# Layer 1's modulation of the context stream only where it is used, and output projections in blocks of 512 columns by 512 rows

## The chip, the cores and the metric

The kernel runs on one core of a Trainium2 chip. The metric is the device time of one execution in microseconds (us). TensorE (PE) multiplies matrices from SBUF into the eight banks of PSUM; VectorE (DVE), ScalarE (ACT) and GpSimd (POOL) work on elements; SyncE (SP) issues the transfers from and to HBM. The order of the instructions on each engine is fixed when the program is built.

## The reference

Two layers of a diffusion backbone work on 256 context tokens and 256 latent tokens of 1024 channels. Of the context, layer 1 uses only what its token mixer reads; the output is the latent stream.

```python
for l in range(DEPTH):                       # DEPTH = 2
    need_ctx = l < DEPTH - 1
    m_l = split(silu(c)     @ w_ada[l] + b_ada[l], 6)    # w_ada[l]: 1024 x 6144
    m_c = split(silu(c_ctx) @ w_ada[l] + b_ada[l], 6)
    h_l = modulate(rms_norm(x,   norm_g[l, 0]), m_l[0], m_l[1])   # h * (1 + scale) + shift
    h_c = modulate(rms_norm(ctx, norm_g[l, 0]), m_c[0], m_c[1])
    y_l, y_c = token_mixer(h_l, h_c, ...)    # ends in merged @ w_out[l], 1024 x 1024
    x = x + m_l[2] * rms_norm(y_l, norm_g[l, 1])
    h_l = modulate(rms_norm(x, norm_g[l, 2]), m_l[3], m_l[4])
    x = x + m_l[5] * rms_norm(relu(h_l @ w_mlp_up[l])**2 @ w_mlp_down[l], norm_g[l, 3])
    if need_ctx:                             # not in layer 1
        ...the same for ctx with m_c[2] to m_c[5]
return x
```

## The kernel before

**Precision.** Each float32 operand of a projection is split in two parts, `hi` (rounded) and `lo` (the rest), and a product takes three matmuls: hi by hi, hi by lo, lo by hi. For weights ACT writes `hi` (line 226) and DVE `lo` (line 227), four pieces of 128x512 for each weight block. A block has 2048 columns in SBUF (1 MB from HBM, two transfers of 512 KB) and there are two block buffers in `whl`; block n+2 is split when block n has been read.

**Two forms of projection.** `mm_cm` (lines 248 to 250) holds weights in the array and moves activations past them: 512 tokens at a time in layer 0, mostly 256 in layer 1. `mm_tm` (lines 260 to 262) holds the activations of one token tile (`tt`, 128 tokens: 0 and 1 are context, 2 and 3 latent) and moves the weights. `tm_out` uses it for `w_out` and for the MLP's second matrix, called the down projection here.

**tm_out.** A block is 1024 rows (8 tiles of `k`) by 256 columns. For each block and each token tile 24 matmuls of 256 columns sum into half a PSUM bank; then DVE adds the result to `y` (line 652), or ACT copies it (655) where it is the first. In a last pass ACT squares it and sums the squares (657) and DVE multiplies by the gate (659). `seqs` lists which token tiles go through which blocks together. When a tile has all its columns, `after` runs: `post` (629 to 633) adds the normalized result to `x`, and, where a next stage follows, `prenorm` (transposes, line 581) and `modulate` (596 to 605) make its input `h`. The MLP goes in four quarters `qd` of 1024 hidden channels: the up projection by `cm_blocks` (its `relu2` at lines 1317 to 1320 ends in a DVE subtraction that writes `lo`), then the down projection, summed over the quarters in `y`.

**Modulation of layer 1.** `w_ada[1]` is worked off during layer 0's MLP: 48 steps (3 groups `g` of 2048 columns, 2 halves, 8 row tiles), two to each weight block. A step loads 512 KB and runs one DVE multiply-add of 128x1024 for each stream (lines 400, 403). After eight steps `ada_sum` sums over the partitions with matmuls against ones (412), transposes (419) and adds the bias. Group 0 holds the first shift and scale, groups 1 and 2 the rest.

**Order.** The program is written in the order of the layers; `high_priority` marks splits and evictions, and a scheduler then sets each engine's order at build time.

## Time and profile before

| | |
|---|---|
| median of 3 runs | 1625.68 us (1623.34 to 1628.14) |
| the profiled execution | 1622.66 us, of which 1620.9 us are its span |
| busy: PE, DVE, ACT, POOL | 1569.2, 1091.5, 782.5, 387.8 us |
| mean TensorE clock granted | 0.986 of full speed |
| transfers | 220.26 MB, mean 136 GB/s |

The span runs from the first to the last instruction. In it, the stages that the change touches are these: `w_out` of layer 0 from 597.5 to 647 us; the four down projections of layer 0 from 697.8, 792.9, 885.9 and 980.5 us on; `w_out` of layer 1 from 1391.8 to 1418.2 us; the four down projections of layer 1 from 1453.0, 1499.0, 1545.1 and 1591.2 us on, the last of which ends the program.

### The profile page before, as it was taken

Reading aid. Unit: us, or ns where it says so; the run is one execution under the profiler, and the core shown is the slowest. Engines: PE = TensorE matmul, PEld = TensorE weight load, DVE = VectorE, ACT = ScalarE, POOL = GpSimd, SP = SyncE. Lnnn points to the kernel's source line nnn. Section 1 sums busy time; section 2 is a strip of 40 time slices with the busy share of each in tenths; the row PEclk is TensorE's granted clock in tenths of the full one; section 3 lists DMA queues with packets and bytes.
Section 4 is the critical chain, followed back from the end, with each engine's and each line's share of the span. In section 5 each row is a group of like instructions: output and inputs, shape, how many; then the busy total and the mean of one; then the engine's idle time right before and its main releaser. Section 6 shows DMA issues by size and latency. Waiting matters only on the chain.

```text
span 1620.9 us, 30093 instructions
## 1 busy us (share of the span) xinstructions
PE 1569.2 (97%) x11806; PEld 1401.7 (86%) x11806; DVE 1091.5 (67%) x1994; ACT 782.5 (48%) x1648; POOL 387.8 (24%) x419
## 2 busy tenths in 40 slices
PE   6999999999999999999999999999998999989998
PEld 4788888887777789888898989999897999989998
DVE  4655544676576578687878756776668788765555
ACT  4443433455444457533323146644455656666554
POOL 1142415050510001310102011364455350211001
PEclk9999999999999999999999999999999999989999
DMA  9723243324332346466556534432434254446662
GB/s 282 230 79 118 80 130 117 92 66 130 129 93 53 117 141 195 147 189 188 173 178 195 156 104 133 129 118 73 124 104 105 66 162 113 156 131 182 183 182 92
DMA packets 234270, 220.26 MB, mean 136 GB/s; under 512 B 24400, under 2 KB 226320, under 8 KB 234128
## 3 DMA queue, kind: packets, MB, share of 16 engines
q1 hardware_dynamic: 234128, 218.34, 45.1%
q8 instruction: 92, 1.51, 0.4%
q14 instruction: 50, 0.41, 0.1%
HBM read 217.26 MB, written 1.05 MB: 135 GB/s over the span
## 4 chain that ended last, share of the span: by engine, by line
PE 84%; DVE 4%; POOL 4%; DMA 2%; ACT 2%; issue 2%; SPq 1%; DVEq 0%; POOLq 0%; ACTq 0%
PE b L248 15%; PE b L249 15%; PE b L250 15%; PE b L260 9%; PE b L261 9%; PE b L262 9%; DMA arf<-in_w_ada_dram 1%; POOL arf L906 1%; PE b L364 1%; POOL arf L796 1%; PE b L1109 1%; PE b L936 1%; PE b L1096 1%; DVE whl L227 1%; PE b L937 1%
## 5 line engine op out<-in xcount | busy, mean ns | idle before, releaser
L227 DVE TENSOR_TENSOR whl<-raw,whl 128x512 fp32r<-128x512 f32 x588 | 431.9, 755 | 213.0 <-ACT whl L226 201.0
L226 ACT CAST whl<-raw 128x512 fp32r<-128x512 f32 x588 | 356.1, 619 | 247.5 <-PE b L262 111.8
L248 PE MATMUL b<-h,whl 128*128 128x512 f32 (+1 forms) x1296 | 448.1, 347 | 1.1 <-ACT arf L951 0.6
L250 PE MATMUL b<-h,whl 128*128 128x512 f32 (+1 forms) x1296 | 445.4, 344 | 0.9 <-DVE whl L227 0.8
L249 PE MATMUL b<-h,whl 128*128 128x512 f32 (+1 forms) x1296 | 444.7, 343 | 0.0
L248 PEld LDWEIGHTS b<-h,whl 128*128 128x128 f32 x1296 | 247.7, 191 | 33.4 <-ACT whl L226 2.1
L250 PEld LDWEIGHTS b<-h,whl 128*128 128x128 f32 x1296 | 246.8, 191 | 29.4 <-issue 1.6
L249 PEld LDWEIGHTS b<-h,whl 128*128 128x128 f32 x1296 | 247.1, 191 | 28.1 <-issue 2.4
L262 PE MATMUL b<-whl,arr 128*128 128x256 f32 x768 | 215.9, 284 | 1.9 <-DVE arr L1320 1.9
L261 PE MATMUL b<-whl,arr 128*128 128x256 f32 x768 | 217.5, 284 | 0.0
L260 PE MATMUL b<-whl,arr 128*128 128x256 f32 x768 | 217.5, 284 | 0.0
L1319 POOL TENSOR_TENSOR arf<-arf 128x256 f32<-128x256 f32 (+1 forms) x68 | 62.3, 916 | 427.7 <-ACT arr L1318 424.1
L260 PEld LDWEIGHTS b<-whl,arr 128*128 128x128 f32 x768 | 147.5, 192 | 1.4 <-DVE arf L652 0.8
L262 PEld LDWEIGHTS b<-whl,arr 128*128 128x128 f32 x768 | 146.8, 192 | 2.1 <-DVE arr L1320 2.1
L261 PEld LDWEIGHTS b<-whl,arr 128*128 128x128 f32 x768 | 147.5, 192 | 0.1
L260 PE MATMUL b<-whl,h 128*128 128x256 f32 x512 | 146.6, 288 | 0.0
L261 PE MATMUL b<-whl,h 128*128 128x256 f32 x512 | 146.0, 286 | 0.0
L262 PE MATMUL b<-whl,h 128*128 128x256 f32 x512 | 144.7, 285 | 0.0
L906 POOL TENSOR_TENSOR arf<-arf,cst 32x256 f32<-32x256 f32 x104 | 94.3, 907 | 192.7 <-ACT arf L951 71.0
L454 POOL TENSOR_TENSOR sm<-sm,nhalf 128x1 f32<-128x1 f32 (+2 forms) x42 | 33.2, 794 | 345.2 <-DVE sm L629 247.2
L403 DVE SCALAR_TENSOR_TENSOR arf<-arf,CA 128x1024 f32<-128x1024 f32 x84 | 109.3, 1345 | 4.8 <-DMA arf<-in_w_ada_dram 4.8
L260 PEld LDWEIGHTS b<-whl,h 128*128 128x128 f32 x512 | 98.6, 193 | 3.2 <-ACT arf L740 0.8
(224 smaller groups left out, 2504.3 us busy)
## 6 DMA issues: line engine op xcount, KB each, us to landing
raw<-in_w_in_dram SPq DMA_DIRECT2D x110, 512.0 KB, 3.9
arf<-in_w_ada_dram SPq DMA_DIRECT2D x80, 512.0 KB, 4.7
raw<-in_w_mlp_down_dram SPq DMA_DIRECT2D x72, 512.0 KB, 3.7
raw<-in_w_mlp_up_dram SPq DMA_DIRECT2D x64, 512.0 KB, 3.9
raw<-in_w_out_dram SPq DMA_DIRECT2D x24, 512.0 KB, 3.6
arf<-in_w_ada_dram SPq DMA_DIRECT2D x32, 256.0 KB, 5.8
raw<-in_w_branch_dram SPq DMA_DIRECT2D x16, 512.0 KB, 4.2
raw<-in_w_in_dram SPq DMA_DIRECT2D x32, 128.0 KB, 3.3
```

Source lines behind the costliest of these rows:

```text
L226: self.behind(ops, lambda: nc.scalar.copy(r32(h), src))
L227: self.split_op = self.behind(ops, lambda: nc.vector.tensor_tensor(out=r32(l), in0=src, in1=h, op=ALU.subtract))
L248: nc.tensor.matmul(ps, wh, xh[:, t0:t0 + n], start=start and k == 0, stop=False)
L249: nc.tensor.matmul(ps, wh, xl[:, t0:t0 + n], start=False, stop=False)
L250: nc.tensor.matmul(ps, wl, xh[:, t0:t0 + n], start=False, stop=stop and k == nk - 1)
L260: nc.tensor.matmul(ps, xh, wh, start=start and k == 0, stop=False)
L261: nc.tensor.matmul(ps, xh, wl, start=False, stop=False)
L262: nc.tensor.matmul(ps, xl, wh, start=False, stop=stop and k == nk - 1)
L403: self.nc.vector.scalar_tensor_tensor(out=a[:, :], in0=raw[:, :], scalar=ca[:, k, s:s + 1], in1=a[:, :], op0=ALU.mult, op1=ALU.add)
L454: self.nc.gpsimd.tensor_tensor(out=r, in0=ms, in1=self.nhalf[:, 0:cols], op=ALU.pow)
L906: nc.gpsimd.tensor_tensor(out=b[o, 0:LAT], in0=x[i], in1=self.cst[i, C_RS:C_RS + LAT], op=ALU.mult)
L1319: nc.gpsimd.tensor_tensor(out=r[:, c], in0=r[:, c], in1=r[:, c], op=ALU.mult)
```

## The change

A block in `tm_out` is now 512 rows (4 tiles of `k`) by 512 columns, again 2048 columns in SBUF. A sum fills a whole PSUM bank and takes two blocks (`kh` 0 and 1): all token tiles of a sequence go through the first block, each in a bank of its own, and then through the second; where `whole` is set (the last columns of layer 1), both blocks are loaded and the tiles go through both in turn. Evictions have 512 columns (`finish`), and the squares of a token are two sums in place of four. For groups 1 and 2 of layer 1's modulation only the latent stream is multiplied, summed and transposed; the loads stay.

```diff
--- before.py
+++ after.py
@@ -135,7 +135,7 @@
         self.oml = const("oml", 8)
         self.nhalf = const("nhalf", 8)
         self.ones = const("ones", 32)
-        self.yss = const("yss", 20)
+        self.yss = const("yss", 12)
         self.sm_t = const("sm", 512)
         self.sm_i = 0
         self.raw = const("raw", RAWS * 1024)
@@ -374,7 +374,7 @@
             while len(raws) < min(n + 1 + ahead, len(todo)):
                 raws.append(self.ada_load(l, *todo[len(raws)]))
             g, half, k = todo[n]
-            self.ada_acc(raws[n], k, acc)
+            self.ada_acc(raws[n], k, acc, 1 if l == DEPTH - 1 and g else 2)
             if k == 7:
                 self.ada_sum(l, g, half, acc)
                 acc.clear()
@@ -389,11 +389,11 @@
             self.nc.sync.dma_start(raw[:, :].rearrange("p (j c) -> p j c", j=4), src)
         return raw
 
-    def ada_acc(self, raw, k, acc):
+    def ada_acc(self, raw, k, acc, streams):
 
         ca = self.CA.rearrange("p (k m) -> p k m", m=32)
         if k == 0:
-            acc += [self.A.get(2) for _ in range(2)]
+            acc += [self.A.get(2) for _ in range(streams)]
         for s, a in enumerate(acc):
             with self.tc.issue_after(self.split_op.ins):
                 if k == 0:
@@ -413,15 +413,16 @@
                                  a[:, j * 256:j * 256 + 256], start=True, stop=True)
             a.free()
         t = self.A.get(1)
-        nc.vector.tensor_copy(t[:, :], ps)
+        n = 2 * len(acc)
+        nc.vector.tensor_copy(t[:, 0:n * 128], ps[:, 0:n * 128])
         p2 = self.mps()
-        for c in range(4):
+        for c in range(n):
             nc.tensor.transpose(p2[:, c * 128:c * 128 + 128], t[:, c * 128:c * 128 + 128], self.ident)
         t.free()
         qs = slice(2 * half, 2 * half + 2)
         out = self.M[l].rearrange("p (s g j q) -> p s g j q", s=2, g=3, j=4)[:, :, g, :, qs]
         bb = self.bT[:, l * 48 + g * 16:l * 48 + g * 16 + 16].rearrange("p (j q) -> p j q", j=4)[:, :, qs]
-        for s in range(2):
+        for s in range(len(acc)):
             nc.vector.tensor_tensor(out=out[:, s], in0=view(p2, s * 256, [(32, 4), (128, 2)]), in1=bb, op=ALU.add)
 
     def ada_done(self, l, g, qs=range(4), p2=None):
@@ -459,7 +460,7 @@
         nc = self.nc
         part = lambda t: t if q is None else t.rearrange("p (a q) -> p a q", a=2)[:, :, q]
         res = []
-        for s in range(2):
+        for s in range(1 if sub and l == DEPTH - 1 else 2):
             S = self.sb[:, ((l * 2 + sub) * 2 + s) * 8:][:, 0:8]
             g = self.prm[:, l * 32 + sub * 16:l * 32 + sub * 16 + 8]
             nc.vector.scalar_tensor_tensor(out=part(S), in0=part(self.mvec(l, s, 3 * sub + 1)), scalar=1.0, in1=part(g),
@@ -638,26 +639,38 @@
 
         nc = self.nc
         junk = self.A.get(1)
-        left = {tt: 4 for tt in y}
-        for tts, blocks in seqs:
-            blks = [(b, self.wblock(w, r0, 8, b * 256, 256)) for b in blocks]
-            for tt in tts:
-                for b, blk in blks:
-                    ps = self.dps()
-                    self.mm_tm(ps[:, 0:256], blk, 8, 0, 256, act, tt)
-                    o = y[tt][:, b * 256:b * 256 + 256]
-                    with self.hp():
-                        src = ps[:, 0:256]
-                        if add:
-                            nc.vector.tensor_tensor(out=o, in0=src, in1=o, op=ALU.add)
-                            src = o
-                        elif not gains:
-                            nc.scalar.copy(o, src)
-                        if gains:
-                            nc.scalar.activation(junk[:, 0:256], src, AF.Square, scale=D ** -0.5,
-                                                 accum_out=yss[tt][:, b:b + 1])
-                            nc.vector.tensor_tensor(out=o, in0=src, in1=gains(tt)[:, b * 256:b * 256 + 256], op=ALU.mult)
-                left[tt] -= len(blks)
+        left = {tt: 2 for tt in y}
+
+        def finish(tt, b, ps):
+            o = y[tt][:, b * 512:b * 512 + 512]
+            with self.hp():
+                src = ps
+                if add:
+                    nc.vector.tensor_tensor(out=o, in0=src, in1=o, op=ALU.add)
+                    src = o
+                elif not gains:
+                    nc.scalar.copy(o, src)
+                if gains:
+                    nc.scalar.activation(junk[:, :], src, AF.Square, scale=D ** -0.5, accum_out=yss[tt][:, b:b + 1])
+                    nc.vector.tensor_tensor(out=o, in0=src, in1=gains(tt)[:, b * 512:b * 512 + 512], op=ALU.mult)
+            left[tt] -= 1
+
+        for tts, halves, whole in seqs:
+            for b in halves:
+                ps = {}
+                order = [(kh, tt) for kh in range(2) for tt in tts]
+                blks = {}
+                if whole:
+                    order = [(kh, tt) for tt in tts for kh in range(2)]
+                    blks = {kh: self.wblock(w, r0 + kh * 512, 4, b * 512, 512) for kh in range(2)}
+                for kh, tt in order:
+                    if kh not in blks:
+                        blks[kh] = self.wblock(w, r0 + kh * 512, 4, b * 512, 512)
+                    if not kh:
+                        ps[tt] = self.dps()
+                    self.mm_tm(ps[tt], blks[kh], 4, 0, 512, act, tt, kt0=kh * 4, start=not kh, stop=kh == 1)
+                    if kh:
+                        finish(tt, b, ps[tt])
             for tt in tts:
                 if gains and left[tt] == 0:
                     after(tt)
@@ -1273,10 +1286,10 @@
         sv = self.scale_vecs(l, 1)
         y = {tt: A.get(2) for tt in tts}
         if not last:
-            seqs = [((0, 1), (b,)) for b in range(4)] + [((2, 3), (b,)) for b in range(4)]
+            seqs = [((0, 1), (0, 1), False), ((2, 3), (0, 1), False)]
         else:
-            seqs = [((2, 3), (0,)), ((2, 3), (1,)), ((2, 3), (2, 3))]
-        yss = {tt: self.yss[:, tt * 5:tt * 5 + 5] for tt in tts}
+            seqs = [((2, 3), (0,), False), ((2, 3), (1,), True)]
+        yss = {tt: self.yss[:, tt * 3:tt * 3 + 3] for tt in tts}
 
         late = []
 
@@ -1355,11 +1368,11 @@
                 if not last:
                     sv = self.scale_vecs(l + 1, 0)
             if last and qd == 3:
-                seqs = [((2, 3), (0,)), ((2, 3), (1,)), ((2, 3), (2, 3))]
+                seqs = [((2, 3), (0,), False), ((2, 3), (1,), True)]
             elif qd == 3:
-                seqs = [((0, 1), (b,)) for b in range(4)] + [((2, 3), (b,)) for b in range(4)]
+                seqs = [((0, 1), (0, 1), False), ((2, 3), (0, 1), False)]
             else:
-                seqs = [(tts, (b,)) for b in range(4)]
+                seqs = [(tts, (0, 1), False)]
             self.tm_out(I["w_mlp_down"][l], qd * 1024, act, y, yss, seqs, qd > 0, gains if qd == 3 else None, after)
             for b in ab.values():
                 b.free()
```

In the order of the instructions the stages keep their sequence. TensorE, first down projection of layer 0 (`b1_85`, `b2_86` are PSUM banks, here of token tiles 0 and 1), before:

```order
L260 MATMUL b2_86<-whl_80,arr_83 128x256
L261 MATMUL b2_86<-whl_80,arr_83 128x256
L260 MATMUL b1_85<-whl_80,arr_83 128x256
L261 MATMUL b1_85<-whl_80,arr_83 128x256
L262 MATMUL b2_86<-whl_80,arr_83 128x256
```

and in the changed kernel, where the first tile hands over to the second after 12 matmuls:

```order
L260 MATMUL b1_85<-whl_80,arr_83 128x512
L261 MATMUL b1_85<-whl_80,arr_83 128x512
L262 MATMUL b1_85<-whl_80,arr_83 128x512
L260 MATMUL b2_86<-whl_80,arr_83 128x512
L261 MATMUL b2_86<-whl_80,arr_83 128x512
L262 MATMUL b2_86<-whl_80,arr_83 128x512
```

Before, the scheduler had threaded the last products of tile 0 among those of tile 1; now each tile's twelve stand together, and the four products with the later hidden channels have moved behind all four tiles' first twelve.

TensorE, a column sum of the modulation's group 1 (`ones` is the operand that sums over partitions) between the first and the second block of a down projection, before:

```order
L262 MATMUL b0_84<-whl_80,arr_83 128x256
L412 MATMUL b6_90<-arf_82,ones_76 32x256 x8
L260 MATMUL b1_85<-whl_80,arr_83 128x256
L261 MATMUL b1_85<-whl_80,arr_83 128x256
L262 MATMUL b1_85<-whl_80,arr_83 128x256
```

and now:

```order
L262 MATMUL b0_84<-whl_80,arr_83 128x512
L412 MATMUL b6_90<-arf_82,ones_76 32x256 x4
L260 MATMUL b1_85<-whl_80,arr_83 128x512
L261 MATMUL b1_85<-whl_80,arr_83 128x512
L262 MATMUL b1_85<-whl_80,arr_83 128x512
```

The place is the same, the sums of one stream are gone.

TensorE, from the end of layer 1's `w_out` to its MLP (lines 581 and 619 transpose the normalized tiles and the next gate; after the change they are 582 and 620), before:

```order
L262 MATMUL b2_86<-whl_80,h_81 128x256
L581 MATMUL b6_90<-cst_61,arf_82 128x128 x4
L581 MATMUL b5_89<-cst_61,arf_82 128x128 x4
L619 MATMUL b6_90<-cst_61,sm_78 128x128 x4
L619 MATMUL b5_89<-cst_61,sm_78 128x128 x4
L581 MATMUL b7_91<-cst_61,arf_82 128x128 x4
L581 MATMUL b4_88<-cst_61,arf_82 128x128 x4
```

and now:

```order
L262 MATMUL b2_86<-whl_80,h_81 128x512
L582 MATMUL b5_89<-cst_61,arf_82 128x128 x4
L582 MATMUL b6_90<-cst_61,arf_82 128x128 x4
L582 MATMUL b7_91<-cst_61,arf_82 128x128 x4
L582 MATMUL b4_88<-cst_61,arf_82 128x128 x4
L620 MATMUL b5_89<-cst_61,sm_78 128x128 x4
L620 MATMUL b6_90<-cst_61,sm_78 128x128 x4
```

The gate's transposes have moved behind the second tile's.

## Rows read from the trace of the kernel before

**Rows 1.** The page: engines, and TensorE's busy tenths over 40 slices.
```profile
PE 1569.2 (97%) x11806; PEld 1401.7 (86%) x11806; DVE 1091.5 (67%) x1994; ACT 782.5 (48%) x1648; POOL 387.8 (24%) x419
...
PE   6999999999999999999999999999998999989998
```

**Rows 2.** Windows of six stretches (columns: stretch, length, busy and count by engine, clock, DMA).
```profile
597.50:647.00 49.50, 49.47 (x402) 48.76 (x401) 41.97 (x81) 34.46 (x84) 5.42 (x6) 1.00 0.59 182
792.90:840.60 47.70, 47.70 (x405) 46.95 (x404) 35.73 (x50) 10.94 (x18) 1.58 (x1) 1.00 0.59 177
980.50:1028.40 47.90, 47.90 (x403) 47.90 (x402) 39.10 (x83) 33.01 (x80) 7.31 (x7) 1.00 0.52 157
1499.00:1522.00 23.00, 23.00 (x194) 23.00 (x193) 14.01 (x25) 10.57 (x19) 0.67 (x1) 1.00 0.61 183
657.40:676.00 18.60, 16.37 (x123) 15.96 (x123) 11.66 (x23) 8.40 (x20) 6.81 (x7) 0.91 0.21 66
1418.20:1427.60 9.40, 4.92 (x24) 3.94 (x24) 7.78 (x20) 6.10 (x15) 2.79 (x4) 0.70 0.18 57
```

**Rows 3.** Groups by line and shape, TensorE: one matmul line of the down projections.
```profile
L260 PE MATMUL b<-whl,arr 128*128 128x256 f32 x768 | 217.5, 284 | 0.0
```

**Rows 4.** Timeline, TensorE: first and last of 192 matmuls of 256 columns (start, duration).
```profile
1499.04 0.28 PE L260 MATMUL b<-whl,arr 128*128 128x256 f32 x1
...
1521.96 0.28 PE L262 MATMUL b<-whl,arr 128*128 128x256 f32 x1
```

**Rows 5.** Timeline, TensorE: first and last of 114 matmuls of 512 columns.
```profile
860.04 0.39 PE L248 MATMUL b<-h,whl 128*128 128x512 f32 x1
...
885.70 0.39 PE L250 MATMUL b<-h,whl 128*128 128x512 f32 x1
```

**Rows 6.** Timeline, TensorE: column sums and transposes of one modulation half, and what follows.
```profile
711.54 1.07 PE L412 MATMUL b<-arf,ones 128*32 128x256 f32 x16
712.54 0.39 PE L260 MATMUL b<-whl,arr 128*128 128x256 f32 x1
...
717.07 0.60 PE L419 MATMUL b<-cst,arf 128*128 128x128 f32 x4
717.43 0.36 PE L261 MATMUL b<-whl,arr 128*128 128x256 f32 x1
```

**Rows 7.** Groups by line and shape, VectorE: the multiply-adds of the modulation.
```profile
L403 DVE SCALAR_TENSOR_TENSOR arf<-arf,CA 128x1024 f32<-128x1024 f32 x84 | 109.3, 1345 | 4.8 <-DMA arf<-in_w_ada_dram 4.8
```

**Rows 8.** Timeline, TensorE: the one wait inside a down projection.
```profile
700.08 0.28 PE L261 MATMUL b<-whl,arr 128*128 128x256 f32 x1
702.23 0.39 PE L262 MATMUL b<-whl,arr 128*128 128x256 f32 x1 [1.86 <-DVE arr L1320]
```

**Rows 9.** Timeline, VectorE: the last multiply-add before the sums at 711.54.
```profile
708.09 1.27 DVE L403 SCALAR_TENSOR_TENSOR arf<-arf,CA 128x1024 f32<-128x1024 f32 x1
```

**Rows 10.** Groups by line and shape, VectorE: PSUM reads of 256 and of 512 columns.
```profile
L652 DVE TENSOR_TENSOR arf<-b,arf 128x256 f32<-128x256 f32 x72 | 30.0, 422 | 29.3 <-PE b L262 27.9
L1167 DVE TENSOR_TENSOR arf<-b,arf 128x512 f32<-128x512 f32 x24 | 16.5, 690 | 20.6 <-PE b L250 20.5
```

**Rows 11.** Groups by line and shape, ScalarE: squares of 256 and of 512 columns.
```profile
L657 ACT ACTIVATE arf<-arf 128x256 f32<-128x256 f32 x24 | 10.0, 415 | 18.2 <-DVE arf L652 18.1
L566 ACT ACTIVATE arf<-arf 128x512 f32<-128x512 f32 x20 | 12.5, 628 | 2.7 <-DVE arf L633 2.7
```

**Rows 12.** Timeline, VectorE: the last result added up, behind the last matmul.
```profile
1614.44 0.42 DVE L652 TENSOR_TENSOR arf<-b,arf 128x256 f32<-128x256 f32 x1 [0.73 <-PE b L262]
```

**Rows 13.** Timeline, VectorE: last splits of a block in layer 0, and in layer 1.
```profile
1005.96 1.28 DVE L227 TENSOR_TENSOR whl<-raw,whl 128x512 fp32r<-128x512 f32 x2
...
1552.05 0.68 DVE L227 TENSOR_TENSOR whl<-raw,whl 128x512 fp32r<-128x512 f32 x1
```

**Rows 14.** Timeline, TensorE: first use of those two blocks.
```profile
1009.42 0.28 PE L260 MATMUL b<-whl,arr 128*128 128x256 f32 x1
...
1556.64 0.28 PE L260 MATMUL b<-whl,arr 128*128 128x256 f32 x1
```

## The prediction

> **What bounds the kernel now.** I read the page first: TensorE is busy 1569.2 of 1620.9 us, and in its strip every slice but the first stands at 8 or more [rows 1]. Then the windows of the stages that the change touches. `w_out` of layer 0, a down projection of layer 0 and one of layer 1 are filled by TensorE to the last hundredths (49.47 of 49.50, 47.70 of 47.70, 23.00 of 23.00 us) at a granted clock of 1.00; DVE is busy 41.97, 35.73 and 14.01 us of the same stretches, ACT less, the DMA engines about 0.6 [rows 2]. So in these stages the kernel lasts as long as TensorE's list, and only two things count: what each matmul takes in a dense row, and what TensorE waits for at the seams. The mean duration in a group of matmuls (284 ns [rows 3]) is not that: they overlap. The spacing of starts is: 192 matmuls of 256 columns start between 1499.04 and 1521.96 us, 22.92 us over 191 steps, 120.0 ns each [rows 4]; 114 matmuls of 512 columns between 860.04 and 885.70 us, 25.66 us over 113 steps, 227.1 ns each [rows 5].
>
> **Wider matmuls.** A line of the three runs 768 times in the down projections [rows 3]; `w_out` adds 4 token tiles x 4 blocks x 8 tiles of k = 128 in layer 0 and 64 in layer 1. That is 960 for each line, 2880 matmuls of 256 columns, which become 1440 of 512. Two old ones take 240.0 ns, one new one 227.1, if activations in the array and weights moving pace like the reverse; nothing in the trace has weights moving 512 wide. For 256 columns both forms exist and both take 120 ns, so I take 227.1 also here. Saved: 1440 x 12.9 ns = 18.6 us. The bounds: nothing, if the new form takes 240.0, and below nothing if it were slower than that, for which no row speaks; upward 1440 x 26.7 = 38 us, if 512 columns took only the 213.3 ns that 512 cycles need at the granted 2.4 GHz. The row of the same width decides.
>
> The two rates split a matmul into 13 ns for the instruction and 0.418 ns for a column, and the first part is what the change halves in number [rows 4, 5]. The Trainium skill (TensorE: Matmul & The Clock Gate, section "Back-to-back issue gap") puts the warm spacing at the columns over 2.4 GHz plus 2.5 ns; by it a pair of 256 takes 218.3 ns and a 512 takes 215.8, and 1440 mergers would bring an estimated 3.6 us. The trace doesn't agree: its 256 columns take 120.0 ns where the page has 109.2, each behind a weight load of its own, so the sum goes by the rows.
>
> **Less modulation.** 32 of the 48 steps (groups 1 and 2) lose one DVE instruction of 1345 ns [rows 7], at most 43 us of DVE time. In the stages where they stand TensorE has no gap (47.70 of 47.70 us [rows 2]), so this brings nothing directly. What it takes from TensorE does: the column sums of a half take 1.00 us (711.54 to the next start) and its transposes 0.36 us, both for two streams [rows 6]. Four halves of the six lose half of that: 4 x 0.68 = 2.7 us. The 48 loads stay, so DMA gains nothing.
>
> **The wait at the first down projection.** The one wait inside these stages is 1.86 us at 702.23 us, on DVE's `lo` of the activations [rows 8]. The new order works through the first four hidden tiles for all four token tiles, 48 x 0.227 = 10.9 us, before it touches the later four, which are made last; this wait goes. Next in line there are the column sums of group 0, which keep both streams. They stand behind those 48 matmuls, which begin about 697.8 us and so end about 708.7, and need the multiply-add that runs from 708.09 to 709.36 us [rows 9]. If DVE's list keeps its times, TensorE waits 0.7 us there. Net gain 1.2 us; bounds 1.9 (DVE comes forward with the rest) and minus 2 (DVE, which in this stretch also waits for loads, comes later by as much as TensorE comes forward).
>
> **Evictions of 512 columns.** Inside a stage they lie beside matmuls. DVE takes 690 ns once for 2 x 422 [rows 10], ACT 628 for 2 x 415 [rows 11], so both get lighter. At a seam the last eviction is on the path: the program ends with the addition behind the last matmul [rows 12], the square, the mean and the write. It gets 0.27 + 0.21 us longer, 0.5 us. At the two seams from `w_out` to the MLP no addition is needed, only the square: 0.2 us each. Together 0.9 us lost. In layer 1 the gate's transposes move behind the second tile's; that seam (TensorE busy 4.92 of 9.40 us, granted clock 0.70 [rows 2]) is paced by the chain through DVE and ACT, so I count this as nothing.
>
> **Blocks.** A two-token block still has 24 matmuls, now 5.45 us instead of 5.76, and the same four splits. The slack: the last split of a block ends at 1552.73 us and its first use is at 1556.64, 3.9 us later; in layer 0's last down projection, where DVE is busiest, it is 1007.24 to 1009.42, 2.2 us [rows 13, 14]. The block's time shrinks by 0.31 us and two evictions cost DVE 0.15 us less each pair. Hidden; if the cover went, each of the 36 blocks that two tiles use (8 in layer 0's `w_out`, 8 in its last quarter, 4 and 16 in layer 1) would show its lateness in full.
>
> **Sum.** 18.6 + 2.7 + 1.2 - 0.9 = 21.6 us. From the profiled execution's 1622.66 us (span 1620.9 and 1.8 around it) that is 1601.1. This execution lies 3.0 us under the median of the runs, 1625.68, by which the same sum gives 1604.1. I predict 1604 us, against the median.
>
> **Rivals.**
> 1. The width brings nothing: moving weights cost by the column, and 512 of them take 240.0 ns. For it: no row shows that form. Against it: at 256 columns the forms agree, and the stationary side, the writes to a full bank and the number of weight loads are like those of the 227.1 ns row. Time: 1604.1 + 18.6 = 1622.7 us, no change that can be measured; the Trainium skill's figure above lies next to it, an estimate of 1619.1 us by that page. Chance 4% for no gain, 2% for some 4 us of it.
> 2. DVE gets behind at the seams of layer 0. TensorE reaches them earlier, and from `w_out` to the MLP it already idles 2.2 us at a clock of 0.91 (16.37 busy of 18.60 us [rows 2]); the column sums of group 0 wait as worked out above, and the last down projection has DVE at 39.10 of 47.90 us with the next layer's normalization in it. If half of what TensorE gains in layer 0 up to there (192 + 768 matmuls x 12.9 ns = 12.4 us) is given back as waiting, 6 us, the time is 1610 us. For it: transposes of the second half now stand together in the list. Against it: DVE's own work there shrinks too. Chance 10%.
> 3. Slower: the splits become the bound of the 36 two-token blocks. One mechanism: with sums of a whole bank both tiles are evicted within one block, behind each other, with 690 ns pieces ahead of the splits on DVE; the next block's `lo` comes late and TensorE waits once for each block. The slack of 2.2 to 3.9 us must be used up first. From 0.6 us of wait a block (36 x 0.6 = 21.6) the gain is gone; at 0.8 us the time is 1604.1 + 28.8 = 1633 us. For it: nothing but DVE's share in layer 0. Against it: the slack. Chance 3%.
> 4. More than forecast: the freed DVE also takes the waits out of layer 0's seams, 2.2 us and the low clock there. The multiply-adds that go come after the first seam, so little speaks for it: 1599 us, 3%.
>
> **How the numbers follow.** The forecast has 78%, of which its own spread (the terms 1.2 and 0.9, and the runs' 1623.34 to 1628.14) is about 1599 to 1609. Rival 2 reaches 1612 and rival 4 lies at the lower end; 1598 to 1612 leaves out about 12% above and below. A measurement of this kernel can tell 0.3%, 4.9 us, from no change. Faster by more: forecast, rivals 2 and 4 and the 2% of rival 1, 93%. Within it: 4%. Slower: 3%.
>
> **What would show it.** In the changed kernel's trace the 512-column matmuls of lines 260 to 262 should start 227 ns apart, 96 of them in 21.8 us in layer 1 where 192 took 22.9, and a down projection of layer 0 should take about 43.6 us of matmuls instead of 46.1. The wait on `lo` at the first down projection should be gone, with less than 1 us in its place before the sums; sums of groups 1 and 2 should take 0.5 us; DVE should lose some 40 us of multiply-adds without a trace on TensorE. Wrong would be a spacing near 240 ns, or waits of TensorE on line 227 at each block.

## The result, and the profile after

The changed kernel takes 1604.93 us (median of 4 runs, 1602.47 to 1605.79); the kernel before took 1624.72 us (median of 4, 1623.34 to 1628.14) beside it. The ratio is 0.9873, with a 95% interval of 0.9853 to 0.9892. The two profiled executions are 1602.47 and 1622.66 us long, with spans of 1600.7 and 1620.9 us and the same mean granted clock, 0.986, so the pair differs by 20.2 us. The page of the changed kernel, its engines and TensorE's strip, to be held against [rows 1]:

```profile
PE 1546.6 (97%) x10326; PEld 1323.4 (83%) x10326; DVE 1045.6 (65%) x1897; ACT 777.4 (49%) x1588; POOL 393.0 (25%) x419
...
PE   6999999999999999999999999999898999989997
```

TensorE has 1480 matmuls fewer and is busy 22.6 us less; DVE is busy 45.9 us less, the share of TensorE is the same. Windows of five of the six stretches of [rows 2] (stretch, length, busy and count by engine, clock, DMA share, GB/s), shifted to where the stages lie now:

```profile
787.60:832.10 44.50, 44.50 (x204) 36.24 (x203) 25.55 (x34) 10.81 (x18) 1.58 (x1) 1.00 0.61 189
967.60:1013.00 45.40, 45.40 (x211) 37.69 (x210) 36.19 (x67) 31.25 (x66) 9.64 (x7) 1.00 0.55 165
1480.90:1502.60 21.70, 21.70 (x99) 17.99 (x98) 13.18 (x21) 11.01 (x20) 0.61 (x1) 1.00 0.62 189
654.70:675.30 20.60, 17.20 (x120) 16.70 (x119) 13.47 (x25) 8.84 (x20) 5.68 (x7) 0.83 0.34 101
1402.30:1412.50 10.20, 4.82 (x25) 4.45 (x24) 8.66 (x23) 7.62 (x19) 3.09 (x4) 0.67 0.16 58
```

The down projections are filled by TensorE as before and are shorter: 44.50 for 47.70, 45.40 for 47.90, 21.70 for 23.00 us. The two seams have become longer, 20.60 for 18.60 and 10.20 for 9.40 us.

The groups by line and shape that answer to [rows 7, 10] (busy, mean ns):

```profile
L403 DVE SCALAR_TENSOR_TENSOR arf<-arf,CA 128x1024 f32<-128x1024 f32 x56 | 76.3, 1385 | 3.5 <-DMA arf<-in_w_ada_dram 3.0
L649 DVE TENSOR_TENSOR arf<-b,arf 128x512 f32<-128x512 f32 x36 | 24.8, 689 | 25.0 <-PE b L262 24.9
```

28 of the 84 multiply-adds are gone (the other 4 of the 32 were each the first step of a half, on another line), and an eviction of 512 columns takes the 690 ns that the older line of that shape had. TensorE's timeline, the first and the last of the 96 matmuls of the second down projection of layer 1 (start, duration), answering to [rows 4]:

```profile
1481.00 0.40 PE L260 MATMUL b<-whl,arr 128*128 128x512 f32 x1
...
1502.56 0.39 PE L262 MATMUL b<-whl,arr 128*128 128x512 f32 x1
```

21.56 us over 95 steps is 226.9 ns each: the rate of [rows 5], with weights as the moving operand. The column sums in the first and in the second down projection of layer 0 and the transposes behind the latter, answering to [rows 6, 8]:

```profile
708.08 1.07 PE L412 MATMUL b<-arf,ones 128*32 128x256 f32 x16
...
798.64 0.64 PE L412 MATMUL b<-arf,ones 128*32 128x256 f32 x8
799.21 0.50 PE L260 MATMUL b<-whl,arr 128*128 128x512 f32 x1
...
804.35 0.38 PE L420 MATMUL b<-cst,arf 128*128 128x128 f32 x2
804.48 0.48 PE L261 MATMUL b<-whl,arr 128*128 128x512 f32 x1
```

With one stream the sums take 0.57 us (798.64 to the next start) and the transposes 0.13, where both streams took 1.00 and 0.36 [rows 6]. At 708.08 no wait is named: in the whole of the first down projection TensorE has none.

By starts of TensorE's matmuls, the span splits so (us; the forecast's part of each stage beside it):

| stage | before | after | difference | forecast |
|---|---|---|---|---|
| start to the last matmul of layer 0's `w_out` | 646.90 | 643.88 | -3.0 | -2.5 |
| from there to the MLP's first matmul of 512 columns | 29.12 | 31.45 | +2.3 | +0.2 |
| four down projections of layer 0 | 192.59 | 179.05 | -13.5 | -12.5 |
| three up projections between them | 137.91 | 136.76 | -1.2 | -1.4 |
| last down projection of layer 0 to the first matmul of layer 1's `w_out` | 363.47 | 364.68 | +1.2 | 0 |
| `w_out` of layer 1 | 26.10 | 24.44 | -1.7 | -1.2 |
| its seam, and the first up projection of layer 1 | 35.08 | 34.14 | -0.9 | +0.2 |
| four down projections of layer 1 | 91.68 | 86.24 | -5.4 | -5.0 |
| three up projections between them | 69.48 | 69.78 | +0.3 | 0 |
| last matmul's start to the end | 6.78 | 8.50 | +1.7 | +0.5 |

The one stage left out, up to the first down projection, has not changed (21.79 and 21.78). The sum of the differences is -20.2 us, of the forecasts -21.7.

### The profile page after: what moved, and what is told of

It reads as the page before. It is cut to its first block, busy times and chain, and to the rows that moved or that the text cites. A ratio compares the mean times of both kernels' runs of the same rounds, so it can differ in the third digit from the quotient of the medians.

```text
span 1600.7 us, 26956 instructions
## 1 busy us (share of the span) xinstructions
PE 1546.6 (97%) x10326; PEld 1323.4 (83%) x10326; DVE 1045.6 (65%) x1897; ACT 777.4 (49%) x1588; POOL 393.0 (25%) x419
## 4 chain that ended last, share of the span: by engine, by line
PE 85%; DVE 5%; POOL 4%; DMA 2%; ACT 2%; issue 2%; SPq 1%; POOLq 0%; DVEq 0%; ACTq 0%
PE b L248 16%; PE b L249 16%; PE b L250 16%; PE b L260 8%; PE b L261 8%; PE b L262 8%; POOL arf L919 1%; PE b L364 1%; DVE whl L227 1%; PE b L1122 1%; PE b L1109 1%; PE b L869 1%; PE b L949 1%; PE b L950 1%; PE b L853 1%
## 5 line engine op out<-in xcount | busy, mean ns | idle before, releaser
L262 PE MATMUL b<-whl,arr 128*128 128x512 f32 x384 | 149.9, 390 | 0.0
L261 PE MATMUL b<-whl,arr 128*128 128x512 f32 x384 | 149.9, 390 | 0.0
L260 PE MATMUL b<-whl,arr 128*128 128x512 f32 x384 | 149.7, 391 | 0.0
L260 PE MATMUL b<-whl,h 128*128 128x256 f32 (+1 forms) x416 | 129.0, 313 | 0.0
L261 PE MATMUL b<-whl,h 128*128 128x256 f32 (+1 forms) x416 | 128.7, 311 | 0.0
L262 PE MATMUL b<-whl,h 128*128 128x256 f32 (+1 forms) x416 | 128.6, 311 | 0.0
L455 POOL TENSOR_TENSOR sm<-sm,nhalf 128x1 f32<-128x1 f32 (+2 forms) x42 | 37.0, 883 | 333.5 <-DVE sm L630 242.5
L809 POOL TENSOR_TENSOR arf<-arf 128x512 f32<-128x512 f32 x56 | 75.8, 1376 | 43.7 <-ACT arf L788 24.1
L260 PEld LDWEIGHTS b<-whl,h 128*128 128x128 f32 x416 | 80.0, 192 | 6.4 <-ACT arf L753 0.8
L260 PEld LDWEIGHTS b<-whl,arr 128*128 128x128 f32 x384 | 72.1, 188 | 15.9 <-issue 1.2
L262 PEld LDWEIGHTS b<-whl,arr 128*128 128x128 f32 x384 | 72.1, 188 | 14.9
L261 PEld LDWEIGHTS b<-whl,arr 128*128 128x128 f32 x384 | 72.1, 188 | 14.5
```

What stands on the lines that cost most here:

```text
L260: nc.tensor.matmul(ps, xh, wh, start=start and k == 0, stop=False)
L261: nc.tensor.matmul(ps, xh, wl, start=False, stop=False)
L262: nc.tensor.matmul(ps, xl, wh, start=False, stop=stop and k == nk - 1)
L455: self.nc.gpsimd.tensor_tensor(out=r, in0=ms, in1=self.nhalf[:, 0:cols], op=ALU.pow)
L809: nc.gpsimd.tensor_tensor(out=kx, in0=kx, in1=view(cur, 1, [(nb - 1, 2), (2, nb // 2), (0, h)]), op=ALU.mult)
```

## Where the seam and the tail went: rows of both kernels

Of the rows of the table that miss by a microsecond or more, two are places where a small loss was forecast and a larger one came: the first seam and the tail. At the seam TensorE's timeline of the changed kernel shows the matmuls around the restart (idle time before in brackets, with what ended it):

```profile
660.56 0.80 PE L248 MATMUL b<-h,arr 128*128 128x256 f32 x2 [3.27 <-ACT h L604]
...
662.28 0.42 PE L250 MATMUL b<-h,arr 128*128 128x256 f32 x1
662.50 0.42 PE L248 MATMUL b<-h,arr 128*128 128x256 f32 x1
```

and of the kernel before:

```profile
661.97 0.51 PE L248 MATMUL b<-h,arr 128*128 128x256 f32 x2 [1.53 <-ACT h L603]
...
663.41 0.38 PE L249 MATMUL b<-h,arr 128*128 128x256 f32 x1 [0.70 <-POOL h L605]
663.63 0.28 PE L250 MATMUL b<-h,arr 128*128 128x256 f32 x1
663.75 0.28 PE L248 MATMUL b<-h,arr 128*128 128x256 f32 x1
```

One long wait of 3.27 us (and one of 0.13 us behind it) stands where two of 1.53 and 0.70 stood, and behind it the matmuls start some 215 ns apart instead of 120. ScalarE's casts say what TensorE waited for. They turn a half of a token tile (four of its eight parts of 128 channels) into the operand `h`. Before:

```profile
660.16 0.62 ACT L603 CAST h<-arf 128x512 fp32r<-128x512 f32 x1
661.30 0.62 ACT L603 CAST h<-arf 128x512 fp32r<-128x512 f32 x1
662.86 1.13 ACT L603 CAST h<-arf 128x512 fp32r<-128x512 f32 x2
```

and after:

```profile
657.22 0.62 ACT L604 CAST h<-arf 128x512 fp32r<-128x512 f32 x1
658.67 0.61 ACT L604 CAST h<-arf 128x512 fp32r<-128x512 f32 x1
659.90 1.12 ACT L604 CAST h<-arf 128x512 fp32r<-128x512 f32 x2
```

The order of the instructions tells the casts apart. Before, they were the first half of tile 2, the first half of tile 3, then the second halves. Now the second half of tile 2 comes second and the first half of tile 3 third. The first matmuls on the latent tokens take both tiles' first half, so they wait for the third cast instead of the second. The granted clock (the number third from the end) shows the rest. The lower of its two levels, 1.2 GHz, reads 0.50. Before, TensorE is at that level for some 3.4 us, from 664.2 to 667.6 us, and after for some 6.8 us, from 660.3, just before the restart, to 667.1. Of each stretch a window:

```profile
664.20:667.55 3.35, 3.35 (x18) 3.35 (x17) 1.22 (x3) 0.00 (x0) 0.00 (x0) 0.50 0.52 160
```

```profile
660.40:667.10 6.70, 6.42 (x28) 6.12 (x29) 2.93 (x4) 0.62 (x2) 1.27 (x1) 0.50 0.52 157
```

By windows of the whole seam the stretch from the transposes to the restart grew by 1.2 us (5.95 to 7.13) and the 92 matmuls behind it by 0.8 (12.61 to 13.42).

At the tail, VectorE's timeline of the changed kernel, to be held against [rows 12]:

```profile
1592.18 1.41 DVE L634 SCALAR_TENSOR_TENSOR arf<-arf,sm 128x512 f32<-128x512 f32 x2 [0.66 <-POOL sm L455]
1593.52 0.68 DVE L649 TENSOR_TENSOR arf<-b,arf 128x512 f32<-128x512 f32 x1
```

The last matmul starts at 1592.20 and is done by about 1592.6, yet tile 3's addition begins at 1593.52: DVE is in tile 2's two updates (L634). Before, the addition waited for TensorE alone. The order of TensorE's instructions shows why tile 2 is late: the scheduler has threaded the last matmuls of tile 2 among those of tile 3, where before all of tile 2's stood ahead of tile 3's.

## The experiments

**The columns, taken apart again.** Every sum of 24 matmuls keeps its block of 512 and its order, but 22 of the 24 are issued as two of 256 columns.

```diff
...
-            nc.tensor.matmul(ps, xh, wl, start=False, stop=False)
...
+                for c in ((0,) if n <= 256 or first or end else (0, 256)):
+                    m = n if n <= 256 or first or end else 256
+                    nc.tensor.matmul(ps[:, c:c + m], x, wt[:, c:c + m], start=first, stop=end)
```

> The changed kernel, with 22 of the 24 matmuls of each sum in the output and down projections issued as two of 256 columns into the same bank: 1320 pairs in place of 1320 matmuls of 512. Blocks, transfers, evictions and modulation are those of the changed kernel. Theory A (a matmul costs about 13 ns beside its columns, and the change gained by issuing half as many): 1320 x 12.9 ns = 17.0 us more than the changed kernel, about 1622 us, spacing 120 ns. Theory B (the gain came from fewer evictions, longer rows in the transfers or the new order): at most 2 us more, about 1605 to 1607 us.

Measured: 1621.03 us (median of 10, 1618.91 to 1624.98), ratio to before 0.998 (0.997 to 0.9989). That is 16.1 us above the changed kernel, 12.2 ns for each of the 1320 pairs. The timeline of TensorE, its last down projection in one row (the row stands for all of its 184 matmuls, 176 of 256 and 8 of 512 columns):

```profile
1587.94 23.12 PE L264 MATMUL b<-whl,arr 128*128 128x512 f32 x184
```

From 1587.94 to the end at 1611.06 it lasts 23.12 us, nearly as before (23.20, from 1591.20 to 1614.40), where the changed kernel needs 21.95. So the gain of the wide projections hangs on the number of matmuls. Longer blocks, order and evictions bring nearly nothing in sum: of the 3.9 us that are left against the kernel before, 2.7 are the modulation by the forecast, which the next two runs bear out, and 1.5 are the 120 matmuls left whole. The Trainium skill (TensorE: Matmul & The Clock Gate, section "Back-to-back issue gap") gives, for a matmul by itself, a gap of 2.5 ns beyond its columns. An estimate by that page for these 1320 pairs is 3.3 us; the runs do not agree with it. For streams in which each matmul has a weight load, as here, the same section of the Trainium skill has other numbers, about 81 ns at 128 columns and 131 ns at 512; the 226.9 ns measured at 512 columns don't agree with these either.

**Each part alone.** The wide projections with both streams kept:

```diff
-            self.ada_acc(raws[n], k, acc, 1 if l == DEPTH - 1 and g else 2)
+            self.ada_acc(raws[n], k, acc, 2)
```

> The changed kernel with both streams in layer 1's modulation, as before the change. Theory A (the DVE time saved there is hidden, only TensorE's sums and transposes count): 4 x 0.68 = 2.7 us more than the changed kernel, about 1607.5 us, and no new waits of TensorE. Theory C (the freed DVE time also shortens waits): 5 us or more, with waits of TensorE on DVE in layer 0's MLP.

and the smaller modulation on the kernel before, whose projections stay at 256 columns (the sums and the transposes run over `len(acc)` streams):

```diff
-            self.ada_acc(raws[n], k, acc)
+            self.ada_acc(raws[n], k, acc, 1 if l == DEPTH - 1 and g else 2)
...
```

> The kernel before with only the modulation's second stream taken out of groups 1 and 2; blocks of 256 columns. Theory A: 2.7 us less than before, about 1622 us, the wait of 1.9 us at the first down projection still there. Theory C: 5 us or more less.

Measured: the first 1606.25 us (median of 4, 1605.42 to 1608.98), ratio to before 0.9891 (0.9874 to 0.9907), 1.3 us above the changed kernel, within what runs differ by. The second 1621.8 us (median of 10, 1619.66 to 1625.53), ratio 0.9986 (0.9976 to 0.9996), 3.1 us below before. The stages say it more sharply. With both streams the second and the third down projection of layer 0 take 45.05 us each where the changed kernel has 44.35 and 44.36, and the three up projections together 138.19 us where it has 136.76: about 0.70 us for each of the four halves. On the kernel before, those two down projections fall from 47.57 to 46.92, 0.65 us. The sums with both streams, TensorE's timeline of the first kernel:

```profile
799.15 1.07 PE L412 MATMUL b<-arf,ones 128*32 128x256 f32 x16
800.15 0.50 PE L260 MATMUL b<-whl,arr 128*128 128x512 f32 x1
```

They take 1.00 us, with no wait ahead of them. And in the second kernel the wait at its first down projection is still there:

```profile
705.90 0.39 PE L262 MATMUL b<-whl,arr 128*128 128x256 f32 x1 [1.86 <-DVE arr L1321]
```

So DVE's share in it has no price of its own: the modulation is worth its sums and transposes on TensorE, and the wait on `lo` was taken away by the other part, the projections.

**The order by blocks, undone at one place.** In layer 0's first down projection each token tile goes through both blocks of hidden tiles before the next:

```diff
-                seqs = [(tts, (0, 1), False)]
+                seqs = [(tts, (0, 1), not last and qd == 0)]
```

> The changed kernel, with each token tile sent through both blocks in turn in layer 0's first down projection, so that the first tile needs all eight hidden tiles at once, as before the change. Theory A (the wait on the lo part went because the first block needs only the first four hidden tiles): a wait of about 2 us on DVE comes back in that stage, 45.3 us become about 47, the whole about 1607 us. Rival: DVE is earlier there anyway since it has less to do, and the stage stays at 45.3 us.

Measured: 1604.85 us (median of 4, 1604.0 to 1606.86), ratio 0.9885 (0.987 to 0.9901). The stage takes 45.75 us instead of 45.06, and the timeline names no wait in it. A miss: no wait on the activations came back. The 0.7 us are other things: two steps of 0.45 and 0.34 us from 700.05, where a step is 0.23, at a weight block whose split on VectorE is late, and the column sums, which run in two lots (at 706.63 and 708.10 us) and cost some 0.3 us more. VectorE's list tells why the wait is gone here too. The subtraction that writes the `lo` waited for, before:

```profile
701.49 0.68 DVE L1320 TENSOR_TENSOR arr<-arf,arr 128x512 fp32r<-128x512 f32 x1
```

in the changed kernel, and in this one:

```profile
697.49 0.68 DVE L1333 TENSOR_TENSOR arr<-arf,arr 128x512 fp32r<-128x512 f32 x1
```

```profile
698.32 0.68 DVE L1333 TENSOR_TENSOR arr<-arf,arr 128x512 fp32r<-128x512 f32 x1
```

Before, it begins 3.68 us behind the first matmul of the stage, in the changed kernel 0.37 and here 1.66 us. So the order by blocks isn't needed for the wait to go; the subtraction itself comes earlier in VectorE's list. Why it was placed earlier, and whether the order by blocks alone would have been enough, no run shows.

**Tile 3 behind tile 2, twice.** Tile 3's first matmul of a sequence may be issued only behind tile 2's last, in both places where layer 1 takes each tile through a block to its end:

```diff
+            with self.tc.issue_after(behind.ins) if behind and k == 0 else nullcontext():
+                nc.tensor.matmul(ps, xh, wh, start=start and k == 0, stop=False)
...
+                                    behind=mm if whole and not kh else None)
```

> The changed kernel, with tile 3's first matmul in the last columns of layer 1 (w_out and the last down projection) held behind tile 2's last, so that the two tiles aren't threaded. The trace of the changed kernel has 8.5 us between the last matmul's start and the end of the span, 1.7 more than before; the addition of tile 3 starts 1.3 us after the last matmul's start, behind tile 2's two late updates on DVE. Theory D (threading made tile 2 late, and DVE does its updates ahead of tile 3's addition): the tail falls to about 7.4 us, 1 us less in all. Theory E (the tail is longer only because 512 columns are evicted at once): no change. The seam from w_out to the MLP in layer 1 should not become longer than 10.2 us.

Measured: 1606.1 us (median of 4, 1605.18 to 1609.98), ratio 0.989 (0.9875 to 0.9905). The tail shrank to 7.61 us as expected, but layer 1's `w_out` grew from 24.44 to 26.17 us. TensorE's timeline there:

```profile
1395.47 0.50 PE L261 MATMUL b<-whl,h 128*128 128x512 f32 x1 [0.30 <-ACT whl L226]
1396.39 0.50 PE L262 MATMUL b<-whl,h 128*128 128x512 f32 x1 [0.41 <-DVE whl L227]
```

It waits for the splits of its weights, which the threading of the two tiles had hidden. The edit put one cost in the place of another, so it was repeated in the last down projection alone (`turns` names the sequence and block whose tiles are held):

```diff
+                                    behind=mm if turn and tt != tts[0] and kh != whole else None)
...
+                        ((1, 1),) if last and qd == 3 else ())
```

> The changed kernel, with tile 3 held behind tile 2 only in the last columns of the last down projection; w_out keeps its threaded order, since holding it there made TensorE wait about 1.6 us for splits and the clock stayed low for a stretch after the seam. Theory D (the threaded tile is what lengthened the tail): 0.9 us less behind the last matmul than the changed kernel, 7.6 us in place of 8.5, no new wait in the last down projection, and everything ahead of it unchanged: about 1604 us. Rival: the last down projection gets waits for splits of its own, as w_out did, and nothing is left of the 0.9 us.

Measured: 1601.56 us (median of 4, 1600.22 to 1601.89), ratio 0.9862 (0.9847 to 0.9877). The last down projection takes 21.57 us, so nothing waits there, and the tail 7.60 instead of 8.50. VectorE's timeline:

```profile
1590.44 1.42 DVE L636 SCALAR_TENSOR_TENSOR arf<-arf,sm 128x512 f32<-128x512 f32 x2 [0.66 <-POOL sm L457]
1592.92 0.69 DVE L651 TENSOR_TENSOR arf<-b,arf 128x512 f32<-128x512 f32 x1 [1.06 <-PE b L263]
```

Tile 2's updates are over before the last matmul, and the addition follows it by 0.42 us. The tail's extra 0.9 us was the threading. The other 0.8 against before are the wider pieces: the last matmul (0.10), the addition and the square (0.48), and the time from the mean to the update (0.26): the update waits for a GpSimd step that takes 0.93 instead of 0.66 us, beside a multiplication on VectorE of 0.68 instead of 0.41 us. The total can't show 0.9 us: it lies 3.4 us under the changed kernel, with intervals of the ratio that overlap.

**The first seam.** Its casts might come in another order because `w_out`'s last matmuls are threaded too. So tile 3's last twelve were held behind tile 2's there as well:

```diff
+        self.tm_out(I["w_out"][l], 0, self.hact, y, yss, seqs, False, gains, after, () if last else ((1, 1),))
```

> The same, and also tile 3's last twelve matmuls of layer 0's w_out held behind tile 2's. In the changed kernel these were threaded, tile 2 ended 2 matmuls before tile 3 where it had ended 10 before, and the stretch from the end of w_out to the first 512-column matmul of the MLP took 31.2 us in place of 29.0. Theory F (tile 2's late end starts both tiles' normalization at once, and this lengthened the seam): 1.4 to 2.2 us of the seam come back, about 1602 us. Rival G (the seam is paced by a split on ScalarE that waits for w_mlp_up's transfer, ahead of the squares in its list): the seam stays at about 31 us.

Measured: 1604.18 us (median of 4, 1600.5 to 1605.9), ratio 0.9875 (0.9852 to 0.9897). The seam lasts 31.44 us, the wait for the cast is 3.39 us: nothing came back, and that theory falls. Then the halves themselves were put in the order that they had before, on top of the kernel with the last projection in turn:

```diff
...
+        for b in range(2):
+            for tt, tiles, yb in pair:
+                ops = [first] if b and tt == 2 else []
...
+                cast = self.behind(ops, lambda: nc.scalar.copy(r32(hi), src))
+                if not b and tt == 3:
+                    first = cast
...
```

> On top of tile 3 held behind tile 2 in the last down projection, only the modulation behind layer 0's w_out changes: the halves of tiles 2 and 3 are issued as first half of tile 2, first half of tile 3, second half of tile 2, second half of tile 3, and ScalarE may cast tile 2's second half only behind tile 3's first. The seam (last matmul of w_out to the first 512-column matmul of the MLP) was 31.2 us in this kernel, 31.45 in the changed kernel, 29.12 before. Theory H (ScalarE's order of the casts costs the 2 us: the first matmul of the latent tokens needs tile 3's first half, which came third): the wait of TensorE for the cast, 3.3 us in the changed kernel, falls to about 1.5 to 2 us, the seam is 29 to 30 us, and the time falls by 1 to 2 us, to about 1600. Theory G (something else paces the restart: the split of the first block of weights on ScalarE, GpSimd's subtraction for the lower part, or the clock behind the wait): the casts come in the new order and the wait for ScalarE is shorter, but the seam stays within 0.5 us of 31.2.

Measured: 1600.85 us (median of 4, 1599.99 to 1603.38), ratio 0.9854 (0.9836 to 0.9871). The seam is 29.31 us. In the six other kernels here with matmuls of 512 columns, with both orders of `w_out`, it lay between 30.58 and 31.45, in the kernel with the pairs apart at 30.39, and before at 29.12. TensorE's timeline at the restart:

```profile
658.96 0.80 PE L248 MATMUL b<-h,arr 128*128 128x256 f32 x2 [2.53 <-ACT h L631]
```

and two windows with the granted clock:

```profile
661.50:663.00 1.50, 1.50 (x12) 1.50 (x11) 0.25 (x1) 0.00 (x0) 0.00 (x0) 0.71 0.38 87
663.00:664.50 1.50, 1.50 (x15) 1.50 (x14) 0.00 (x0) 0.00 (x0) 0.00 (x0) 1.00 1.05 362
```

The wait fell by 0.74 us, less than expected, and the full clock is back at about 662.4, 3.4 us behind the restart instead of 6.6. Against its own base, 31.17 us, the seam is 1.9 us shorter. But not all of that need be the order: two of the six kernels have the old order of the casts and yet only 3.4 us at the lower clock. The kernel that held tile 3 twice is one of them, with this restart and this window of the lower clock:

```profile
660.09 0.50 PE L248 MATMUL b<-h,arr 128*128 128x256 f32 x2 [3.31 <-ACT h L606]
```

```profile
661.25:664.50 3.25, 3.05 (x14) 3.06 (x15) 1.36 (x2) 0.00 (x0) 0.14 (x1) 0.50 0.83 259
```

The seams of those two, 30.58 and 30.76 us, are 1.3 and 1.5 us longer than this one with as much of the lower clock. So the order of the casts is shown as the cause of some 1.3 of the 2.3 us; the rest goes with a longer stretch at the lower clock, which came and went between executions of the same order. The total agrees with that without showing it alone: it lies 4.1 us under the changed kernel, with intervals of the ratio that overlap. This is the fastest version that was run.

## Why the prediction was right, point by point

- **Wider matmuls, 18.6 us: right.** 226.9 ns were measured where 227.1 were taken from the row of the same width. Issuing the pairs apart cost 16.1 us for 22 of 24 matmuls, which is 17.6 for all. Rival 1 falls, in both its forms.
- **Less modulation, 2.7 us: right.** 0.65 to 0.70 us for each of four halves, by both kernels with one part alone; nothing from DVE itself.
- **The wait at the first down projection, net 1.2 us: the size was off, and the reason is not shown.** The wait of 1.86 us went, but the order by blocks, to which the prediction put it down, could be undone without the wait coming back: DVE's list did not keep its times, and the `lo` waited for is written 3.3 us earlier in the stage. Nor did 0.7 us come in the wait's place, since DVE came forward there too: its last multiply-add ahead of the sums starts at 704.93 us, 3.2 us before them, where [rows 9] had it 3.5 us before sums that stood 2.8 us later in their stage. The stage fell by 4.6 us, of which 2.5 are width; the 2.1 left lie a little over this step's upper bound of 1.9.
- **Evictions at seams, 0.9 us lost: mis-sized, and this is where the forecast lost most.** The step "only the square: 0.2 us each" priced an instruction's length and took the order around it as given. The order changed: at the first seam the casts, and with them the stretch at the lower clock, for +2.3 us in place of +0.2, and at the tail the threading, for +1.7 in place of +0.5. Of the first, rival 2 had the place but not the mechanism (DVE was not late, ScalarE's list was in another order), and 2.3 of its 6 us. Rival 4 falls: the waits at that seam grew.
- **The seam of layer 1, +0.2 us for the square and nothing for the moved transposes: off by 1.1 us in the other direction.** The seam itself grew by 0.7 us, and the stage behind it shrank by 1.7 us; it begins at full clock now. Before, a piece of it:

```profile
1426.00:1427.50 1.50, 0.55 (x3) 0.14 (x1) 1.47 (x5) 0.85 (x3) 0.00 (x0) 0.50 0.00 0
...
1430.50:1432.00 1.50, 1.50 (x9) 1.50 (x9) 1.50 (x4) 1.50 (x4) 0.00 (x0) 0.50 0.13 14
```

and after:

```profile
1408.50:1410.00 1.50, 1.50 (x9) 1.50 (x8) 1.43 (x5) 0.31 (x2) 0.00 (x0) 0.50 0.00 0
...
1411.50:1413.00 1.50, 1.10 (x8) 0.66 (x6) 1.43 (x4) 1.50 (x5) 0.67 (x1) 1.00 0.00 0
```

  Before, TensorE paused for 1.07 us between the transposes and the first matmul at 1427.62, and the clock stayed at 1.2 GHz until about 1432. After, the transposes of the tiles and of the gate stand together, the pause is 0.40 us, and the clock is at 2.4 GHz before the stage starts at 1412.50. All ten kernels fall in these two groups: in six the transposes stand together and the stage takes 23.7 us; in four (before, the small modulation alone, the pairs apart, and tile 3 held in layer 1's `w_out`) the gate's stand between the tiles', and it takes 25.0 to 25.3. No run changed that order alone, so this cause is supported by ten kernels but not isolated.
- **Blocks: right.** TensorE waits for no split in any wide block of the changed kernel. Rival 3 falls here, though its mechanism is real: in layer 1's `w_out` it appeared as soon as the two tiles were no longer threaded.
- **The stretch from layer 0's last down projection to layer 1's `w_out`, +1.2 us: put at nothing.** The prediction priced no seam there; rival 2 had named the place, with the next layer's normalization in it. TensorE's waits in the changed kernel:

```profile
1013.85 0.39 PE L249 MATMUL b<-h,whl 128*128 128x256 f32 x1 [0.31 <-POOL h L606]
...
1033.44 0.38 PE L248 MATMUL b<-h,whl 128*128 128x256 f32 x1 [0.33 <-ACT arf L753]
```

  and GpSimd's subtractions that write `lo` of the next layer's input, before (the second of two) and after (both):

```profile
1024.64 1.29 POOL L605 TENSOR_TENSOR h<-arf,h 128x512 fp32r<-128x512 f32 x1 [6.48 <-ACT h L603]
```

```profile
1007.92 5.87 POOL L606 TENSOR_TENSOR h<-arf,h 128x512 fp32r<-128x512 f32 x2 [8.39 <-PE b L262]
```

  Before, GpSimd was done 2.4 us ahead of the stage's last matmul (1028.31), the two subtractions 8.5 us apart; now they stand together and end 0.9 us behind it (1012.92). The wait for them costs some 0.6 us with the steps around it, the second place 0.4 us more than before (a wait of 0.33 for 0.23, and a short one on GpSimd behind it), the wider last matmul 0.1. The 256th matmul of this stretch starts 32.1 us behind the down projection's last in all seven kernels with matmuls of 512 columns, 31.3 us with the pairs apart, and 31.0 us in the kernel before and in the one with the small modulation alone: the loss came with the projections. What lies behind it in this stretch took 332.4 to 334.2 us from kernel to kernel, with no order to it.

The pair of profiles shows 20.2 us where the sum had 21.6. The misses are larger than that and cancel: +2.1, +1.2 and +1.2 us at the first seam, at the tail and behind layer 0's last down projection, against -1.1 behind layer 1's seam, -1.0 in the down projections of layer 0 and smaller ones. That 1604 us meets 1604.93 so closely is in part luck: besides these, the forecast counted from a median of 1625.68 us, and the four runs beside the changed kernel have 1624.72, by which the gain is 19.8 us.

## What to carry to other kernels

Where TensorE is full, count its instructions: the spacing of starts in a dense row of each width, not the mean duration, gives what merging them brings; the spacing taken from the old row held here to 0.2 of 227 ns. Work taken from an engine that no one waits for brought only what it issued on the full engine. When a change rebuilds the lists by a scheduler, price the seams by the order in which the engines will do the work there, and look for what the first instruction of the next stage needs: a cast that came third instead of second cost more than a microsecond, where a longer instruction had been priced at 0.2.

## What was not expected of the hardware

At the first seam the length of the wait does not fix what the clock does behind it. With waits of 1.53 and 0.70 us, or of 2.53, TensorE ran at 1.2 GHz for some 3.4 us; with a long wait of 3.31 or 3.40 us and one of 0.6 us behind it, in two kernels, for 3.4 us too; and with 3.23 to 3.54 us, in four other kernels with the same order of the casts, for 6.8 us. The seam was 30.58 and 30.76 us long in the two, 31.17 to 31.45 in the four, so one execution prices it no closer than 0.9 us. What decides between the two lengths no run shows.
